# One pool of eight PSUM banks for the whole program, its banks handed out in turn, and the last gated rows split two at a time

## The chip, the cores and the metric

The kernel runs on one core of one Trainium2 chip. The metric is the device time of one execution in microseconds (us). A core has five engines with queues of their own: TensorE (PE; its weight loads are listed as PEld), VectorE (DVE), ScalarE (ACT), GpSimd (POOL) and SyncE (SP, which here only issues transfers). Matmuls write to PSUM, an accumulator memory of eight banks of 128 x 512 fp32 words; ACT and DVE read the results from there.

## The reference

Two layers over two batches of frames: a prompt of 512 frames of one new stream, and 16 new frames of each of 8 running streams (128 rows), together 640 rows of width 2048 in fp32. Layer 0 is stick-breaking attention with 16 heads of 128 (the running streams also see 512 cached frames); layer 1 is gated linear attention (GLA) with 4 heads, keys of 256 and values of 512, whose recurrent state is updated. Cut to what matters:

```
for layer i in (0, 1):
    shift, scale, gate = split(c @ w_ada[i] + b_ada[i], 3)
    h = rmsnorm(x, norm_g[i]) * (1 + scale) + shift
    i = 0:  q, k, v, z = split(h @ w_in0, 4);  o = stick_breaking(q, k, v)
            y = (o * silu(z)) @ w_out0
    i = 1:  q, k, v, r, a = split(h @ w_in1);  g = log_sigmoid(a @ w_a2 + b_a) / 16
            per chunk:  b = cumsum(g);  q_in = q * exp(b)
                        o = tril(q_in @ (k * exp(-b)).T) @ v + q_in @ S
                        S = exp(b_last) * S + (k * exp(b_last - b)).T @ v
            o = o * rsqrt(mean(o * o) + EPS) * g_out
            y = (o * silu(r)) @ w_out1
    x = x + gate * y
y = rmsnorm(x, final_norm_g)
```

The new keys and values of layer 0 and the final states of layer 1 are outputs too.

## The kernel before, in words

All large products are made with operands split in a high and a low half (fp32r): `halves` casts the high half on ACT (line 134) and subtracts it on DVE (line 135); each product is then three matmuls, high by high, high by low and low by high.

TensorE runs in the order in which the program is written (`manual_schedule(engines={PE})`); the other engines' orders come from the Tile scheduler, which plays the program in a timeline model, except in two stretches where they too are as written. What is written in which order on TensorE is decided by a small planner in the program: `Side` holds lanes (generators), and `drive` runs one piece of the main matmuls, then lets the lanes whose waiting time is over put their own matmuls between. A lane says with `step(wait, tp=, z=)` how long it waits and how many banks it takes; `pe["now"]` counts modelled time. Neither knows about real banks.

The stages, with the names that share the eight banks in each (`share_banks`):

1. adaLN and the input projection of layer 0 (`six`, `by_sevens`, matmuls on line 591; evacuations on line 597): mm=5, z=1, tp=2.
2. Attention of layer 0 (`prompt_lane`, `sample_lane`) between the matmuls of the gate projection (`plain`, line 650) and of the output projection (`share`, line 696; evacuations on lines 701 and 704): mm=2, z=2, tp=4.
3. The rest of layer 0's output projection and the input projection of layer 1: mm=5, z=1, tp=2.
4. GLA attention, again between `plain` (line 650) and `share` (line 696): mm=2, z=1, tp=5.
5. The last columns of layer 1's output projection (`hs_gemm512`, line 365, then line 2088) and the final norm: mm=8.

`bank(tag)` gives a tile of one bank. `share_banks` closes the PSUM pool of the old stage and opens another; within a pool each name is one tag with as many buffers as the stage gives it, and the scheduler chooses a free buffer for each tile.

In stage 4 three lanes run: `decays` (line 1669 matmuls), `prompt_lane` (4 heads x 4 chunks of 128 frames) and `sample_lane`. For each chunk the prompt lane takes a tp tile o and accumulates in it over several pieces (`mm3`, line 1579): attention weights by values, then two groups of query by state. Between them it takes other tp tiles: `update` (line 1579; scaled on ACT, line 1792) and `leave`, which transposes the previous chunk's output (line 1628). When o is complete, `normed` squares it on ACT (line 1604), `rstd_of` computes the root on DVE (line 232) and POOL (line 234), and `scaled_by` scales o on ACT (line 1608), which is the last read of o's bank. The sample lane accumulates in the z bank and takes a tp tile for each of 16 state updates of a head (line 1928, read on DVE, line 1930).

At the start of stage 5, six of the gated rows (kt 10 to 15) are loaded from DRAM and split; rows 8 and 9 were split in stage 4. The block of 8 rows is used in four pairs, each with a pair of weight rows, ten groups of three matmuls for each pair.

Of the kernel before, what the change touches and what calls it, by code (L numbers as in the profile page):

```python
# [8 lines left out]
F32 = mybir.dt.float32  # L9
# [6 lines left out]
P = 128  # L16
# [25 lines left out]
def hybrid_step_kernel(ctx: ExitStack, tc: tile.TileContext, A: dict, O: list):  # L42
    nc = tc.nc
    PS = bass.MemoryType.PSUM
# [9 lines left out]
    def by(l, r):  # L54

        n = r.free_size()
        if l.dtype == F32R:
            pe["now"] += n / 2400 + 0.0133
        elif l.free_size() <= 32:
            pe["now"] += n / pe["quad"] + 0.01  # L60
        else:
            pe["now"] += n / 600 + 0.005
        return r
# [6 lines left out]
    def load(out, in_):  # L70
        nc.sync.dma_start(out=out, in_=in_)

    def store(out, in_):
        nc.sync.dma_start(out=out, in_=in_)
# [10 lines left out]
    banks = ctx.enter_context(ExitStack())  # L85
# [2 lines left out]
    l0 = ExitStack()  # L88
    ad = l0.enter_context(tc.tile_pool(name="ad", bufs=1, reuse_waits="tile"))

    psum = {}

    def share_banks(**bufs):

        banks.close()
        psum["pool"] = banks.enter_context(tc.tile_pool(name="ps", bufs=1, space=PS))
        psum["bufs"] = bufs

    def bank(tag):
        return psum["pool"].tile([P, 512], F32, tag=tag, name=f"ps_{tag}", bufs=psum["bufs"][tag])  # L100

    share_banks(mm=5, z=1, tp=2)


# [28 lines left out]
    def halves(hi, lo, x, e=None):  # L133
        nc.scalar.copy(hi, x)  # L134
        (e or dve).tensor_tensor(lo, x, hi.bitcast(F32), op=ALU.subtract)  # L135
# [13 lines left out]
    def wraw(src, a, n):  # L149
        r = wp.tile([P, 1024], F32, tag="wr", name="wr", bufs=WR)[:, :a * n]  # L150
        load(r.rearrange("p (a n) -> p a n", a=a), src)
        return r
# [4 lines left out]
    def wpiece(src, a, n):  # L157

        return wsplit(wraw(src, a, n), a)
# [68 lines left out]
    def rstd_of(pool, ss, n, name):  # L228

        w = ss.shape[1]  # L230
        ms = pool.tile([P, w], F32, tag=name + "_ms", name=name + "_ms")
        dve.tensor_scalar(ms, ss, 1.0 / n, EPS, op0=ALU.mult, op1=ALU.add)
        r = pool.tile([P, w], F32, tag=name + "_r", name=name + "_r")
        nc.gpsimd.tensor_tensor(r, ms, mhalf[:, :w], op=ALU.pow)
        return r
# [26 lines left out]
    def slot(n, shape=(P, T), dt=F32R, name="h"):  # L262
        return hp.tile(list(shape), dt, tag=f"t{n}", name=name)
# [9 lines left out]
    class Side:  # L273
# [19 lines left out]
        def add(self, gen):  # L293
            self.lanes.append([gen, None])
            self.next(self.lanes[-1])
# [46 lines left out]
    side = Side()  # L342

    def drive(*gens):
        for g in gens:
            for _ in g:
                side.tick()

    def hs_gemm512(hT, w, n0, evac, mid=None, toks=range(TOK), piece=wpiece, k0=0, nk=KT):

        acc = {a: bank("mm") for a in toks}
        src = w.rearrange("(kt p) n -> p kt n", p=P)
        for pc in range(nk // 2):
            if pc == min(2, nk // 2 - 1) and mid is not None:
                mid()
            for k2 in range(2):
                hT[k0 + 2 * pc + k2]
            wh, wl = piece(src[:, k0 + 2 * pc:k0 + 2 * pc + 2, n0:n0 + 512], 2, 512)
            for a in toks:
                c = slice(P * a, P * a + P)  # L360
                for k2 in range(2):
                    kt = k0 + 2 * pc + k2
                    h, lo = hT[kt]
                    for l, r, first, last in ((h, wh, True, False), (h, wl, False, False), (lo, wh, False, True)):
                        mm(acc[a], l[:, c], by(l[:, c], r[:, k2, :]), start=kt == k0 and first,  # L365
                           stop=kt == k0 + nk - 1 and last)
                    if k2 == 0:
                        yield
                if pc == nk // 2 - 1:
                    evac(a, acc[a])  # L370
                yield

    def gate_bc(pool, i, c, bufs=2):

        g = pool.tile([P, 2, 512], F32, tag="gate_bc", name="gate_bc", bufs=bufs)
        cs = slice(512 * c, 512 * c + 512)
        load(g[:, 0, :], gate_d[i][0, cs].partition_broadcast(P))
        for b in range(NB):
            load(g[NT * b:NT * b + NT, 1, :], gate_d[i][1 + b, cs].partition_broadcast(NT))
        return g  # L380
# [542 lines left out]
    with tc.tile_pool(name="kp", bufs=2, reuse_waits="tile") as kp, \  # L923
# [12 lines left out]
        later = at.tile([P, 2], F32, name="later", bufs=1)  # L936
# [313 lines left out]
    with tc.tile_pool(name="o0", bufs=1, reuse_waits="tile") as po, ExitStack() as only_d:  # L1250
# [161 lines left out]
        r = wp.tile([P, 1024], F32, tag="wr", name="wr", bufs=WR)[:, :256].rearrange("p (k n) -> p k n", k=KT)  # L1412
# [77 lines left out]
        n = 0  # L1490
# [13 lines left out]
        r, wa2 = (rows_in.tile([P, GH * 256], t, tag=n, name=n)[:96] for n, t in (("wa2r", F32), ("wa2", F32R)))  # L1504
# [15 lines left out]
    w_out1 = A["gla_w_out"][0]  # L1520
    og1 = {}
# [499 lines left out]
    with tc.tile_pool(name="o1", bufs=1, reuse_waits="tile") as po:  # L2021
        ss4 = po.tile([P, TOK, 4], F32, name="ss4f")
        gf = po.tile([P, D], F32, name="gf")
        ring3["pool"] = po
        for kt in range(10, 16):
            r = po.tile([P, T], F32, tag="rows", name="og_in", bufs=6)
            load(r, og_d[kt // 4][:, kt % 4, :])
            n = 20 + 2 * kt % 12
            og1[kt] = [slot(n + e) if kt < 14 else po.tile([P, T], F32R, name=f"og{e}{kt}") for e in range(2)]
            halves(*og1[kt], r)  # L2030
        got = {}

        def fetch_x1(c):
            if c == 0:
                load(gf, A["final_norm_g"].partition_broadcast(P))
            xs = []
            for a in range(TOK):
                xs.append(po.tile([P, 512], F32, tag="xc", name="x1", bufs=8))
                load(xs[a], x1_d[a][:, 512 * c:512 * c + 512])
            got[c] = xs, gate_bc(po, 1, c)  # L2040

        def add(a, c, pt):
            cs = slice(512 * c, 512 * c + 512)
            xs, g = got[c]
            y = y_t[a, c]
            dve.tensor_tensor(y, pt, y, op=ALU.add)
            dve.tensor_tensor(y, y, g[:, a // 4, :], op=ALU.mult)
            dve.tensor_tensor(y, y, xs[a], op=ALU.add)
            junk = po.tile([P, 512], BF16, tag="junk", name="junk", bufs=1)
            act(junk, y, AF.Square, accum_out=ss4[:, a, c:c + 1])  # L2050
            if c < 3:
                dve.tensor_tensor(y, y, gf[:, cs], op=ALU.mult)
                return
            ss = po.tile([P, 1], F32, tag="ssf", name="ssf", bufs=2)
            dve.tensor_reduce(out=ss, in_=ss4[:, a, :], axis=mybir.AxisListType.X, op=ALU.add)
            r = rstd_of(po, ss, D, "fin")
            dst = y_p[0, P * a:P * a + P, :] if a < 4 else y_s.rearrange("b t d -> (b t) d")
            dve.scalar_tensor_tensor(y, y, r, gf[:, cs], op0=ALU.mult, op1=ALU.mult)
            store(dst[:, cs], y)
            for n in range(3):  # L2060
                x = y_t[a, n]
                if n < 2:
                    act(x, x, AF.Copy, scale=r)
                else:
                    dve.tensor_scalar(x, x, r, None, op0=ALU.mult)
                store(dst[:, 512 * n:512 * n + 512], x)

        def piece(src, a, n):
            t = parts.pop(0) if parts else split(first.pop(0)) if first else None
            return [x.rearrange("p (a n) -> p a n", a=2) for x in t] if t else wpiece(src, a, n)  # L2070

        kept = []
        for c in range(3):
            drive(hs_gemm512(og1, w_out1, 512 * c, lambda a, pt: add(a, c, pt), lambda: fetch_x1(c), piece=piece,
                             k0=8, nk=8))
        for i in range(4):
            r = wraw(w_of(2 + i // 2, 3, i % 2), 2, 512)
            h, lo = (po.tile([P, 1024], F32R, name=f"{n}{i}") for n in ("kh", "kl"))
            halves(h, lo, r)
            kept.append([t.rearrange("p (a n) -> p a n", a=2) for t in (h, lo)])  # L2080
        fetch_x1(3)
        for a in range(TOK):
            acc = bank("mm")
            for n in range(8):
                wh, wl = kept[n // 2]
                h, lo = (x[:, P * a:P * a + P] for x in og1[8 + n])
                for l, r, start, stop in ((h, wh, True, False), (h, wl, False, False), (lo, wh, False, True)):
                    mm(acc, l, by(l, r[:, n % 2, :]), start=n == 0 and start, stop=n == 7 and stop)  # L2088
            add(a, 3, acc)
# [27 lines left out]
```

## Time and profile before

| what | value |
|---|---|
| time, median of 3 runs | 2473.24 us (2471.8 to 2477.05) |
| time of the profiled execution | 2472.03 us |
| its span, first to last instruction | 2470.1 us |
| granted TensorE clock | 0.995 of full speed |
| busy: PE, PEld | 2408.5 us (98%), 2141.9 us (87%) |
| busy: DVE, ACT, POOL | 1581.7 us (64%), 993.3 us (40%), 156.6 us (6%) |
| HBM read, written | 410.05 MB, 89.13 MB |

The stages in the profiled execution run from 0 to about 919, to 1386, to 1945, to 2348 and to 2470 us. Columns of rows of the timeline: start in us, duration in us, engine, source line, operation, tiles as out<-in, shapes and count; in brackets the engine's idle time before the row and what ended it. Rows of the view of stretches give the length, the busy time and instruction count of PE, PEld, DVE, ACT and POOL, then the granted clock, the share of time of the transfer engines, and GB/s. Buffer numbers are left out of names: all tiles of one name look alike.

### The profile page before, as it was taken

What the parts mean: (1) busy time and instruction counts of PE and PEld (TensorE: products, weight loads), DVE (VectorE), ACT (ScalarE), POOL (GpSimd) and SP (SyncE); (2) the same over time, 40 slices, a digit from 0 to 9 for tenths busy, and PEclk for the clock granted to TensorE, in tenths of its full rate; (3) what the DMA queues carried; (4) which work ended last, traced back from release to release, by engine and by line L of the source; (5) the groups of instructions that cost most, each with busy time, mean ns of one, the idle gap of its engine ahead of it and who ended that gap; (6) DMA issues with size and microseconds to landing.
All of it is one profiled execution on the core that took longest, in us unless ns stands there. A gap on an engine that the chain in (4) does not pass through costs nothing.

```text
span 2470.1 us, 44598 instructions
## 1 busy us (share of the span) xinstructions
PE 2408.5 (98%) x17817; PEld 2141.9 (87%) x17817; DVE 1581.7 (64%) x2580; ACT 993.3 (40%) x1711; POOL 156.6 (6%) x405
## 2 busy tenths in 40 slices
PE   7999999999999999999999999999999999999998
PEld 4689999999999999888887767999999989977776
DVE  5765655555556656766776578766676566676556
ACT  4432222222223335555544245433333555565223
POOL 0010000000000000000000010000000132332000
PEclk8999999999999999999999999999999999999999
DMA  9966666766664348777774564444434678976634
GB/s 344 370 218 213 210 216 199 239 210 225 210 197 128 109 145 274 259 241 235 254 235 147 187 234 129 136 123 125 134 111 114 175 247 264 303 261 224 220 115 149
DMA packets 477841, 502.12 MB, mean 203 GB/s; under 512 B 26618, under 2 KB 386434, under 8 KB 477506
## 3 DMA queue, kind: packets, MB, share of 16 engines
q1 hardware_dynamic: 449042, 440.80, 56.2%
q0 software_dynamic: 14432, 46.67, 5.5%
q10 hardware_dynamic: 14160, 11.80, 1.4%
q8 instruction: 140, 2.29, 0.4%
q14 instruction: 67, 0.55, 0.1%
HBM read 410.05 MB, written 89.13 MB: 202 GB/s over the span
## 4 chain that ended last, share of the span: by engine, by line
PE 85%; DVE 4%; ACT 3%; DMA 2%; issue 1%; POOL 0%; SPq 0%; ACTq 0%; POOLq 0%; DVEq 0%
PE ps_mm L591 43%; PE ps_mm L696 11%; PE ps_mm L650 10%; PE ps_mm L365 3%; PE ps_tp L1100 2%; PE ps_tp L1579 2%; PE ps_tp L1152 1%; PE ps_tp L1056 1%; PE ps_z L1032 1%; PE ps_z L180 1%; PE ps_mm L2088 1%; PE ps_z L1114 1%; PE ps_z L222 1%; PE ps_tp L677 1%; PE ps_mm L515 1%
## 5 line engine op out<-in xcount | busy, mean ns | idle before, releaser
L591 PE MATMUL ps_mm<-sums,wh 128*128 128x320 f32 x2752 | 613.6, 311 | 1.5 <-ACT wh L134 1.5
L591 PEld LDWEIGHTS ps_mm<-sums,wh 128*128 128x128 f32 x2752 | 458.0, 188 | 10.4 <-issue 7.4
L591 PE MATMUL ps_mm<-h,wh 128*128 128x320 f32 x2064 | 461.4, 311 | 0.8 <-DVE u L597 0.8
L591 PE MATMUL ps_mm<-sums,wl 128*128 128x320 f32 x1376 | 425.2, 309 | 0.7 <-DVE wl L135 0.7
L135 DVE TENSOR_TENSOR wl<-wr,wh 128x1024 fp32r<-128x1024 f32 x193 | 236.2, 1225 | 211.1 <-ACT wh L134 208.1
L591 PEld LDWEIGHTS ps_mm<-h,wh 128*128 128x128 f32 x2064 | 343.2, 188 | 15.7 <-issue 11.0
L134 ACT CAST wh<-wb 128x1024 fp32r<-128x1024 f32 x170 | 178.4, 1049 | 431.8 <-PE ps_mm L591 368.2
L134 ACT CAST wh<-wr 128x1024 fp32r<-128x1024 f32 x193 | 202.5, 1050 | 324.8 <-PE ps_mm L591 186.8
L591 PE MATMUL ps_mm<-h,wl 128*128 128x320 f32 x1032 | 318.9, 309 | 0.0
L650 PE MATMUL ps_mm<-h,wh 128*128 128x320 f32 x1152 | 263.5, 316 | 3.5 <-DVE out L597 2.4
L591 PEld LDWEIGHTS ps_mm<-sums,wl 128*128 128x128 f32 x1376 | 258.3, 188 | 1.0 <-DVE wl L135 1.0
L135 DVE TENSOR_TENSOR wl<-wb,wh 128x1024 fp32r<-128x1024 f32 x170 | 207.8, 1222 | 51.0 <-ACT wh L134 50.6
L650 PEld LDWEIGHTS ps_mm<-h,wh 128*128 128x128 f32 x1152 | 192.0, 188 | 17.9 <-issue 8.9
L696 PE MATMUL ps_mm<-wh,ogh 128*128 128x512 f32 x450 | 196.8, 437 | 6.2 <-ACT y L704 3.0
L591 PEld LDWEIGHTS ps_mm<-h,wl 128*128 128x128 f32 x1032 | 193.8, 188 | 0.0
L650 PE MATMUL ps_mm<-h,wl 128*128 128x320 f32 x576 | 177.9, 309 | 0.0
L696 PE MATMUL ps_mm<-wh,ogl 128*128 128x512 f32 x450 | 177.0, 393 | 0.3 <-DVE ogl L135 0.3
L696 PE MATMUL ps_mm<-wl,ogh 128*128 128x512 f32 x450 | 177.0, 393 | 0.2 <-DVE wl L135 0.2
L696 PEld LDWEIGHTS ps_mm<-wh,ogh 128*128 128x128 f32 x450 | 84.9, 189 | 34.4 <-issue 15.1
L650 PEld LDWEIGHTS ps_mm<-h,wl 128*128 128x128 f32 x576 | 108.2, 188 | 0.0
L696 PEld LDWEIGHTS ps_mm<-wh,ogl 128*128 128x128 f32 x450 | 84.5, 188 | 20.2 <-DVE ogl L135 0.7
L515 PE MATMUL ps_mm<-wh,h 128*128 128x512 f32 x252 | 90.7, 415 | 5.6 <-ACT h L134 4.0
(370 smaller groups left out, 3719.6 us busy)
## 6 DMA issues: line engine op xcount, KB each, us to landing
ar<-in_w_ada_dram SPq DMA_DIRECT2D x128, 512.0 KB
wb<-in_sb_w_in_dram SPq DMA_DIRECT2D x82, 512.0 KB
ar<-in_w_ada_dram SPq DMA_DIRECT2D x128, 256.0 KB
kc<-in_cache_sb_k_dram SPq DMA_DIRECT2D x64, 512.0 KB
vc<-in_cache_sb_v_dram SPq DMA_DIRECT2D x64, 512.0 KB
wr<-in_gla_w_in_dram SPq DMA_DIRECT2D x51, 512.0 KB
wb<-in_gla_w_in_dram SPq DMA_DIRECT2D x45, 512.0 KB
wr<-in_sb_w_in_dram SPq DMA_DIRECT2D x44, 512.0 KB
```

What stands on the lines that cost most here:

```text
L134: nc.scalar.copy(hi, x)
L135: (e or dve).tensor_tensor(lo, x, hi.bitcast(F32), op=ALU.subtract)
L180: mm(acc[32 * q:32 * q + 32, :w], cT[:, kt + m, :], by(cT[:, kt + m, :], rs[m // each][:, m % each, q, :]), start=kt + m == 0, stop=kt + m ...
L222: mm(acc[32 * j:32 * j + 32, :256], cT[:, kt + m, :], by(cT[:, kt + m, :], r[:, 256 * j:256 * j + 256]), start=kt + m == 0, stop=kt + m == ...
L365: mm(acc[a], l[:, c], by(l[:, c], r[:, k2, :]), start=kt == k0 and first, stop=kt == k0 + nk - 1 and last)
L515: mm(acc[a], l, by(l, r[:, e, :]), start=j == 0 and e == 0 and begun, stop=j == 7 and e == 1 and last)
L591: mm(acc, l[:, k, :], by(l[:, k, :], r), start=start and k == 0 and first, stop=k == 7 and last, skip_group_check=True)
L650: mm(acc[nt], l[:, k, :], by(l[:, k, :], r), start=k0 == 8 and k == 0 and first, stop=k0 == 0 and k == 7 and last)
L677: turn_block(tp[:, c:c + P], block(out[hh][:, t0:t0 + P]), ident)
L696: mm(acc, l, by(l, r[:, e, :]), start=i == 0 and e == 0 and first, stop=i == 1 and e == 1 and last)
L1100: turn_block(tp[:, P * c:P * c + P], block(kc[:, c, P * hh:P * hh + P]), ident)
L1579: mm(out, l[a], by(l[a], r[b]), start=start and n == 0, stop=stop and n == 2, skip_group_check=True)
```

## The change

The PSUM pool is opened once, before the first stage, and never closed. It has eight tags, b0 to b7, of one buffer each. `psum["last"]` holds the banks in the order of their last use, the one used longest ago first. `share_banks` only gives each name so many banks, from the front of that list, and `bank(tag)` takes the name's banks in turn. In stage 5 the loads of the six rows stay where they are; two rows are split there, and two more after the fifth and after the fifteenth group of three matmuls of the first block. The other steps of the loop are as in `drive`.

```diff
-    psum = {}
+    psum = {"pool": banks.enter_context(tc.tile_pool(name="ps", bufs=1, space=PS)), "last": list(range(8)), "of": {}}
 
     def share_banks(**bufs):
 
-        banks.close()
-        psum["pool"] = banks.enter_context(tc.tile_pool(name="ps", bufs=1, space=PS))
-        psum["bufs"] = bufs
+        free = list(psum["last"])
+        psum["of"] = {tag: [free.pop(0) for _ in range(n)] for tag, n in bufs.items()}
 
     def bank(tag):
-        return psum["pool"].tile([P, 512], F32, tag=tag, name=f"ps_{tag}", bufs=psum["bufs"][tag])
+        own = psum["of"][tag]
+        own.append(own.pop(0))
+        psum["last"].remove(own[-1])
+        psum["last"].append(own[-1])
+        return psum["pool"].tile([P, 512], F32, tag=f"b{own[-1]}", name=f"ps_{tag}")
...
         ring3["pool"] = po
+        later = []
         for kt in range(10, 16):
             r = po.tile([P, T], F32, tag="rows", name="og_in", bufs=6)
             load(r, og_d[kt // 4][:, kt % 4, :])
             n = 20 + 2 * kt % 12
             og1[kt] = [slot(n + e) if kt < 14 else po.tile([P, T], F32R, name=f"og{e}{kt}") for e in range(2)]
-            halves(*og1[kt], r)
+            later.append((og1[kt], r))
+
+        def next_rows():
+            for _ in range(2):
+                if later:
+                    two, r = later.pop(0)
+                    halves(*two, r)
+
+        next_rows()
...
         for c in range(3):
-            drive(hs_gemm512(og1, w_out1, 512 * c, lambda a, pt: add(a, c, pt), lambda: fetch_x1(c), piece=piece,
-                             k0=8, nk=8))
+            for n, _ in enumerate(hs_gemm512(og1, w_out1, 512 * c, lambda a, pt: add(a, c, pt), lambda: fetch_x1(c),
+                                             piece=piece, k0=8, nk=8)):
+                if n % 10 == 4:
+                    next_rows()
+                side.tick()
```

## The prediction

> **What bounds the kernel now.** I read the page first (shares, then the chain that ended last), then the busy time by stage, then the timeline of TensorE around each change of stage and around the accumulators of the last-but-one stage.
>
> ```profile
> span 2470.1 us, 44598 instructions
> PE 2408.5 (98%) x17817; PEld 2141.9 (87%) x17817; DVE 1581.7 (64%) x2580; ACT 993.3 (40%) x1711; POOL 156.6 (6%) x405
> PE 85%; DVE 4%; ACT 3%; DMA 2%; issue 1%; POOL 0%; SPq 0%; ACTq 0%; POOLq 0%; DVEq 0%
> ...
> 1945.20:2347.70 402.50, 396.39 (x2292) 341.19 (x2292) 244.93 (x420) 210.96 (x389) 99.57 (x181) 1.00 0.77 250
> ```
>
> TensorE is the bound: it is busy 2408.5 of 2470.1 us. It runs in the order in which the program is written, so a wait at its head stops everything behind it, and a microsecond of waiting is a microsecond of time unless a later wait shrinks by as much. The last row is the GLA attention stage (time, then busy time of PE, PEld, DVE, ACT, POOL): PE stands for 402.50 - 396.39 = 6.1 us there. The change adds and removes no matmul, no transfer and no vector work. It can only move waits, and those are of two kinds: the waits at the four changes of stage, and the waits for a bank inside a stage.
>
> **The change, part 1: the pool is not closed at a change of stage.**
>
> ```profile
> 921.04 0.53 PE L650 MATMUL ps_mm<-h,wh 128*128 128x320 f32 x2 [1.75 <-DVE out L597]
> ...
> 1387.04 0.47 PE L696 MATMUL ps_mm<-wh,ogh 128*128 128x512 f32 x1 [0.88 <-DVE y L701]
> ...
> 1945.86 0.53 PE L650 MATMUL ps_mm<-h,wh 128*128 128x320 f32 x2 [0.68 <-DVE out L597]
> ...
> 2349.36 0.47 PE L365 MATMUL ps_mm<-wh,ogh 128*128 128x512 f32 x1 [1.47 <-DVE y L701]
> ...
> 1386.81 1.22 DVE L135 TENSOR_TENSOR s<-wr,s 128x1024 fp32r<-128x1024 f32 x1
> ...
> 1388.49 0.62 PE L696 MATMUL ps_mm<-s,ogh 128*128 128x512 f32 x2
> ```
>
> Columns of these rows: start, us, engine, line, tiles; in brackets the idle time before it and what ended it. Each is the first matmul of a new stage, and each waits for the last read of the old stage's last bank. With one pool, share_banks hands the names the banks used longest ago first, so the first matmul finds a bank that was read long before. I remove all four waits, 1.75 + 0.88 + 0.68 + 1.47 = 4.8 us, and ask what is late next. At the second change it is a weight: the low half "s" is ready at 1386.81 + 1.22 = 1388.03, and its matmul is the eighth of the stage, at about 1388.7 now (the row at 1388.49 holds the seventh and another). So about 0.6 us of the 0.88 remain. At the other three I know of no late operand: the first weights are split several microseconds before. I take 4.5 us; ends 0 (another operand is late at each) and 4.8.
>
> **Part 2: which bank a tile gets inside a stage.** Before, a name such as tp had five buffers of one tag, and a new tile could have whichever was free. After, bank() takes the names' banks strictly in turn, each a tag with one buffer. For tiles that are used for the same short time nothing changes. In the GLA attention stage one tile is not short: the prompt lane's output accumulator "o" (name tp, L1579), which lives over three later groups of matmuls, the square, the power on POOL and the scaling on ACT (L1608), and only then is free. With tp=5 taken in turn, the fifth tp tile after o gets o's bank, whatever else is free. How that falls for one o:
>
> ```profile
> 2176.96 0.62 PE L1579 MATMUL ps_tp<-v,aTh 128*128 128x512 f32 x2
> ...
> 2178.35 0.39 PE L1928 MATMUL ps_tp<-vst,kst 128*128 128x512 f32 x1
> ...
> 2179.45 0.62 PE L1579 MATMUL ps_tp<-v,krh 128*128 128x512 f32 x2
> ...
> 2180.14 0.40 PE L1928 MATMUL ps_tp<-vst,kst 128*128 128x512 f32 x1
> ...
> 2183.78 0.39 PE L1579 MATMUL ps_tp<-S1h,qcl 128*128 128x512 f32 x1
> 2184.01 0.39 PE L1928 MATMUL ps_tp<-vst,kst 128*128 128x512 f32 x1
> ...
> 2185.13 0.49 PE L1628 MATMUL ps_tp<-ident,on 128*128 128x128 f32 x3
> ...
> 2188.10 0.57 POOL L234 TENSOR_TENSOR on_r<-on_ms,mhalf 128x1 f32<-128x1 f32 x1
> ...
> 2190.46 0.69 ACT L1608 ACTIVATE on<-ps_tp,on_r 128x512 f32<-128x512 f32 x1
> ```
>
> o opens at 2176.96 and gets its last matmul at 2183.78. The next tp tiles open at 2178.35, 2179.45, 2180.14, 2184.01 and 2185.13: the fifth is the transpose of L1628. It starts now without a wait, although o is read until 2190.46 + 0.69 = 2191.15, so it has another bank now. In turn it would stand 2191.15 - 2185.13 = 6.0 us, and on TensorE all of L1628, the sample lane's L1928 and the filler matmuls of L650 or L696 stand behind it; ACT, DVE and POOL wait for their outputs.
>
> I went through the 16 o's of the prompt lane so, counting five tp tiles on from each. Eight of the 16 (heads x chunks) meet their own release. The first and the last of the eight:
>
> ```profile
> 2008.27 0.39 PE L1579 MATMUL ps_tp<-S1h,qcl 128*128 128x512 f32 x1
> ...
> 2011.15 0.62 PE L1579 MATMUL ps_tp<-v,krh 128*128 128x512 f32 x2
> ...
> 2011.67 0.69 ACT L1608 ACTIVATE on<-ps_tp,on_r 128x512 f32<-128x512 f32 x1
> ...
> 2265.44 0.39 PE L1579 MATMUL ps_tp<-S1h,qcl 128*128 128x512 f32 x1
> ...
> 2266.95 0.48 PE L1928 MATMUL ps_tp<-vst,kst 128*128 128x512 f32 x1
> ...
> 2269.00 0.69 ACT L1608 ACTIVATE on<-ps_tp,on_r 128x512 f32<-128x512 f32 x1
> ```
>
> With today's releases the eight waits would be 1.2, 5.1, 1.8, 1.0, 3.7, 4.5, 6.0 and 2.7 us, in sum 26.0, at 2011, 2023, 2038, 2084, 2097, 2109, 2185 and 2267 us. That is the upper end. The release can come earlier than today, because a standing TensorE sends ACT, DVE and POOL no new work, and their queues are filled in another order when the wait is known. The hold, from the end of o's last matmul to the end of L1608, is 3.7 us in the first of the rows, 3.9 in the last, 7.0 in the long one. The shortest in the stage:
>
> ```profile
> 1993.87 0.39 PE L1579 MATMUL ps_tp<-v,aTl 128*128 128x512 f32 x1
> ...
> 1995.85 0.69 ACT L1608 ACTIVATE on<-ps_tp,on_r 128x512 f32<-128x512 f32 x1 [0.87 <-POOL on_r L234]
> ```
>
> There it is 1996.54 - 1994.26 = 2.3 us. From o's last matmul to the fifth tile are 2.5, -0.2, 3.5, 2.5, 0.9, 0.7, 0.9 and 1.1 us in the eight, so a hold of 2.3 us everywhere would leave waits of 0, 2.5, 0, 0, 1.4, 1.6, 1.4 and 1.2, in sum 8: the lower end. I take a hold of 3.8 us, that of the first and last rows, in which little but the chain itself stands: 1.3 + 4.0 + 0.3 + 1.3 + 2.9 + 3.1 + 2.9 + 2.7 = 18.5 us. The z accumulator of the sample lane has its own bank as before; the mm banks were taken in turn of release before and stay near that. In the other stages I find no tile that would come before its bank is read, so nothing is charged there.
>
> What might shrink by as much: after a stall ACT and DVE have caught up, so later waits of PE in this stage can be shorter. They are small:
>
> ```profile
> PE ps_mm L696 <- ACT y L704: 3.0, 3, 1.9
> ...
> PE ps_mm L650 <- ACT pl L1539: 1.0, 1, 1.0
> ```
>
> (Us in total, times, longest.) I give back 1 us of these 4; ends 0 and 4.
>
> **The clock after a stall.** One long stall is in the trace:
>
> ```profile
> 1466.81 0.50 PE L515 MATMUL ps_mm<-wh,h 128*128 128x512 f32 x1 [3.03 <-ACT h L134]
> ...
> 1468.00:1471.40 3.40, 3.40 (x8) 2.68 (x9) 2.64 (x9) 0.90 (x3) 0.55 (x1) 0.51 0.09 34
> 1471.40:1475.40 4.00, 4.00 (x21) 3.06 (x20) 3.39 (x8) 3.54 (x10) 0.00 (x0) 1.00 0.13 45
> ```
>
> After 3.03 us of idle the granted clock is 0.51 for 3.4 us, in which 8 matmuls start, against 21 in the 4.0 us behind: the slow 3.4 us cost about 1.6 us (at 0.5 of the clock half of the time is lost, at most 1.7). The 1.75 us of idle at 921 caused no such row. Of my eight stalls, five are 2.7 to 4.0 us; I charge two such drops, 3.2 us; ends 0 and 8 (five). The Trainium skill, TensorE: Matmul & The Clock Gate, Part 1, states a free-running activity window of about 3.4 us, after an idle one of which the clock halves. The drop's length in the trace agrees, though its idle time was a little shorter than that; by the page's rule read strictly only my one stall of 4.0 us would drop the clock, and the sum would be 1.6 us lower.
>
> **Part 3: the last gated rows two at a time.** Rows 10 and 11 are split (one ACT cast and one DVE subtraction for each row) where all six were; rows 12 to 15 are written into the first column block, after groups 5 and 15. No instruction is added. They are needed at the third and fourth weight pair. In the block, matmuls of the second pair begin at 2356.28, those of the third about 6.8 us later, and DVE idles between:
>
> ```profile
> 2356.28 0.39 PE L365 MATMUL ps_mm<-wh,h 128*128 128x512 f32 x1
> ...
> 2357.57 1.23 DVE L135 TENSOR_TENSOR wl<-wr,wh 128x1024 fp32r<-128x1024 f32 x1 [6.49 <-ACT wh L134]
> ```
>
> A pair of rows costs under 2 us on each engine, inside 6.49 us of DVE's idle time, so I charge 0; without that cover it would be at most 2 us. No queue is moved past a transfer: the six loads stay where they are.
>
> **The sum**, against the profiled execution's own 2472.03 us (span 2470.1; the median of the three runs is 2473.24, 1.2 above): -4.5 + 18.5 + 3.2 - 1 = +16.2, so 2488.2 profiled and about 2489 us in the median, slower by 0.65%.
>
> **Rivals.**
> - *Only the first part shows: the waits inside the stage do not come.* For it: the change keeps every count of banks, and the removed waits are plain in four rows. It decides if o's release can come 3 us sooner than in the rows, at less than a 1 us hold, or if the bank in turn is not o's. Against it: a hold of 2.3 us is the shortest seen. Time: 2473.2 - 4.5 = 2468.7, less 0.18%; up to 2467 if caught-up engines shorten further waits. This is faster or, by the bound of 0.2% (4.9 us, about what a measurement of this kernel can tell from no change), the same. 0.14.
> - *Short holds:* the eight waits come at the lower end, without a drop of the clock: -4.5 + 8 - 1 = +2.5, 2476 us, the same within 0.2%. It decides if the holds fall below 2.6 us. For it: only the chain square, DVE, POOL, ACT is then queued. Against it: POOL's queue holds transfers for the state in front of the power, which wait for landings, not for TensorE. 0.10.
> - *Full holds and the clock:* today's releases and five drops: -4.5 + 26 + 8 = +29.5, 2503 us. The queues of ACT and POOL keep today's order. 0.13.
> - *The change of stage gains nothing* since another operand is late at each: +20.7, 2494 us. 0.05.
>
> **How the numbers follow.** The forecast as summed has the remaining 0.58. Predicted: 2489. The range reaches from the short holds with a margin to most of the full ones, 2473 to 2501, and leaves out the first rival and the far end of the third, about 0.2; the forecast's own range, from the choices of hold between 3 and 4.6 us, is 2481 to 2496. Slower by over 0.2%: forecast 0.58, third 0.13, fourth 0.05, together 0.76. Within 0.2%: short holds 0.10 and half of the first rival, 0.17 in all. Faster: 0.07.
>
> **What would show it.** Right: in the timeline the first matmuls of L650 (twice), L696 and L365 start with no idle time behind L597 and L701; in the waits of PE in the GLA attention stage new rows ps_tp (L1628, L1928, L1579) waiting for ACT on L1608, eight or so, 1 to 6 us each; the stage takes some 16 to 20 us longer; granted clock below 1.00 in slices behind the longest. Wrong: no row of PE waiting for L1608, or the stage's PE idle time still near 6 us; or a new wait in the last stage on the split rows (L365 behind ACT og or h), which would make part 3 cost.

## The result, and the profile after

The changed kernel is slower: 2504.34 us in the median (2500.42 to 2505.31) against 2474.55 us for the kernel before beside it (2471.80 to 2477.05), a ratio of 1.0119 with an interval of [1.0104, 1.0133]. The forecast was 2489 us with a range to 2501: the sign and the eight waits came as said, the size did not. The profiled execution of the changed kernel took 2503.78 us, its span is 2501.7 us (31.6 more than before), its granted clock 0.988 (0.995 before). TensorE's order is the same in both, matmul for matmul, so the delay can be read at each of the 17817 matmuls. At the end of the GLA attention stage it is already over 30 us. Line numbers of the changed kernel are three higher here: L1608 of before is L1611, L1628 is L1631.

The GLA attention stage, from its first matmul (L650, then L653) to the first of the last stage (L365, then L368), in the view of stretches, before and after:

```profile
1945.86:2349.36 403.50, 396.58 (x2293) 341.20 (x2293) 245.87 (x422) 212.51 (x391) 99.57 (x181) 1.00 0.77 249
```
```profile
1945.49:2381.09 435.60, 405.60 (x2295) 347.45 (x2293) 245.74 (x421) 212.08 (x391) 101.16 (x181) 0.98 0.73 231
```

The stage is 435.60 - 403.50 = 32.1 us longer, and the row splits that in two. TensorE is idle for 30.00 us where it was idle for 6.92 (23.1 more), and the same matmuls keep it busy 9.0 us longer, at a granted clock of 0.98. What it waited for (us in total, times, longest):

```profile
PE ps_tp L1631 <- ACT on L1611: 10.4, 3, 5.2
PE ps_tp L1931 <- ACT on L1611: 7.3, 2, 4.7
PE ps_tp L1900 <- DVE kc L1895: 3.9, 1, 3.9
PE ps_tp L1582 <- ACT on L1611: 3.6, 3, 1.7
PE ps_mm L699 <- DVE y L704: 1.5, 4, 0.7
PE ps_mm L699 <- ACT y L707: 1.5, 2, 1.1
...
PE ps_tp L1594 <- DVE k L1698: 0.8, 1, 0.8
```

The three rows that end on L1611, the scaling of o, are new: eight waits, 21.3 us. In the timeline they stand at the eight matmuls that the forecast named, and at no other:

```profile
2011.99 0.50 PE L1582 MATMUL ps_tp<-v,krh 128*128 128x512 f32 x1 [1.10 <-ACT on L1611]
...
2028.71 0.80 PE L1931 MATMUL ps_tp<-vst,kst 128*128 128x512 f32 x1 [4.70 <-ACT on L1611]
...
2047.28 0.50 PE L1582 MATMUL ps_tp<-v,krh 128*128 128x512 f32 x1 [1.66 <-ACT on L1611]
...
2095.76 0.50 PE L1582 MATMUL ps_tp<-v,krh 128*128 128x512 f32 x1 [0.87 <-ACT on L1611]
...
2112.59 0.69 PE L1631 MATMUL ps_tp<-ident,on 128*128 128x128 f32 x2 [3.68 <-ACT on L1611]
...
2129.38 0.44 PE L1631 MATMUL ps_tp<-ident,on 128*128 128x128 f32 x2 [1.53 <-ACT on L1611]
...
2210.71 0.69 PE L1631 MATMUL ps_tp<-ident,on 128*128 128x128 f32 x2 [5.19 <-ACT on L1611]
...
2300.61 0.50 PE L1931 MATMUL ps_tp<-vst,kst 128*128 128x512 f32 x1 [2.58 <-ACT on L1611]
```

Four stretches run at half of the clock, three behind the long ones of these waits and the last behind the wait for kc:

```profile
2026.20:2033.00 6.80, 4.29 (x16) 4.15 (x17) 1.44 (x3) 0.69 (x1) 2.74 (x5) 0.50 0.91 302
2111.50:2118.30 6.80, 5.71 (x22) 3.71 (x22) 1.90 (x3) 1.35 (x2) 1.92 (x4) 0.50 0.92 278
2210.50:2213.90 3.40, 3.19 (x12) 3.10 (x13) 2.18 (x3) 0.15 (x1) 0.86 (x2) 0.50 0.51 173
2227.60:2231.00 3.40, 3.40 (x10) 2.62 (x9) 2.94 (x6) 2.17 (x4) 1.32 (x2) 0.50 1.01 358
```

TensorE is busy 4.29 + 5.71 + 3.19 + 3.40 = 16.6 us in them; half of that, 8.3 us, is lost, and makes up nearly all of the 9.0 us of longer busy time.

The changes of stage came right too: the first matmuls of the four later stages carry no bracket now, and one new wait follows the first of them:

```profile
920.82 0.46 PE L653 MATMUL ps_mm<-h,wh 128*128 128x320 f32 x2
...
930.37 0.42 PE L653 MATMUL ps_mm<-h,wl 128*128 128x320 f32 x1 [1.18 <-DVE wl L138]
...
1387.01 0.39 PE L699 MATMUL ps_mm<-wh,ogh 128*128 128x512 f32 x1
...
1945.49 0.46 PE L653 MATMUL ps_mm<-h,wh 128*128 128x320 f32 x2
...
2381.09 0.39 PE L368 MATMUL ps_mm<-wh,ogh 128*128 128x512 f32 x1
```

So far this is a coincidence of places and of times. That the turn causes the loss, and what makes a wait long, took experiments.

### The profile page after: what moved, and what is told of

The parts are those of the page before. It is cut to its first block, busy times and chain, and to the rows that moved or that the text cites. A ratio compares the mean times of both kernels' runs of the same rounds, so it can differ in the third digit from the quotient of the medians.

```text
span 2501.7 us, 44596 instructions
## 1 busy us (share of the span) xinstructions
PE 2419.7 (97%) x17817; PEld 2151.4 (86%) x17817; DVE 1582.8 (63%) x2580; ACT 994.4 (40%) x1711; POOL 157.9 (6%) x405
## 4 chain that ended last, share of the span: by engine, by line
PE 81%; DMA 4%; DVE 4%; ACT 3%; issue 2%; POOL 0%; SPq 0%; ACTq 0%; POOLq 0%; DVEq 0%
PE ps_mm L594 42%; PE ps_mm L699 10%; PE ps_mm L653 8%; PE ps_mm L368 3%; PE ps_tp L1103 2%; PE ps_tp L1582 2%; PE ps_tp L1155 1%; PE ps_tp L1059 1%; PE ps_z L1035 1%; PE ps_z L183 1%; PE ps_mm L518 1%; PE ps_mm L2103 1%; PE ps_z L1117 1%; PE ps_z L225 1%; PE ps_tp L680 1%
## 5 line engine op out<-in xcount | busy, mean ns | idle before, releaser
L594 PEld LDWEIGHTS ps_mm<-sums,wh 128*128 128x128 f32 x2752 | 458.2, 188 | 10.4 <-issue 7.4
L653 PE MATMUL ps_mm<-h,wh 128*128 128x320 f32 x1152 | 265.7, 318 | 1.0 <-ACT pl L1542 1.0
L653 PEld LDWEIGHTS ps_mm<-h,wh 128*128 128x128 f32 x1152 | 194.3, 190 | 15.7 <-issue 8.7
L699 PE MATMUL ps_mm<-wh,ogh 128*128 128x512 f32 x450 | 197.2, 438 | 4.1 <-DVE y L704 2.2
L653 PE MATMUL ps_mm<-h,wl 128*128 128x320 f32 x576 | 179.1, 311 | 1.2 <-DVE wl L138 1.2
L699 PE MATMUL ps_mm<-wh,ogl 128*128 128x512 f32 x450 | 177.5, 394 | 0.3 <-DVE ogl L138 0.3
L699 PE MATMUL ps_mm<-wl,ogh 128*128 128x512 f32 x450 | 177.4, 394 | 0.0
L699 PEld LDWEIGHTS ps_mm<-wh,ogh 128*128 128x128 f32 x450 | 85.3, 190 | 31.2 <-issue 13.3
L653 PEld LDWEIGHTS ps_mm<-h,wl 128*128 128x128 f32 x576 | 109.3, 190 | 1.4 <-DVE wl L138 1.4
L699 PEld LDWEIGHTS ps_mm<-wh,ogl 128*128 128x128 f32 x450 | 84.8, 188 | 20.4 <-DVE ogl L138 0.7
```

The source lines that it names most:

```text
L594: mm(acc, l[:, k, :], by(l[:, k, :], r), start=start and k == 0 and first, stop=k == 7 and last, skip_group_check=True)
L653: mm(acc[nt], l[:, k, :], by(l[:, k, :], r), start=k0 == 8 and k == 0 and first, stop=k0 == 0 and k == 7 and last)
L699: mm(acc, l, by(l, r[:, e, :]), start=i == 0 and e == 0 and first, stop=i == 1 and e == 1 and last)
```

## The experiments

The theory: the loss comes from banks handed out in turn, which meet the bank that o holds. Rival 1: the pool that lives for the whole program, or the moved splits, cost. Rival 2: the other order that the scheduler gave to ScalarE, VectorE and GpSimd costs, and the bank waits are only its sign. All ratios are against the kernel before, run beside on the same chip. "Stage" is the length of the GLA attention stage between the same two matmuls as above, "idle" TensorE's idle time in it, "scaling" its waits for the scaling of o, and for the copy where there is one.

| kernel | median, us | before beside it, us | ratio, interval | stage, us | idle, us | scaling, us |
|---|---|---|---|---|---|---|
| before | | | | 403.5 | 6.9 | 0 |
| changed | 2504.34 | 2474.55 | 1.0119 [1.0104, 1.0133] | 435.6 | 30.0 | 21.3 |
| rows only | 2476.74 | 2476.52 | 1.0002 [0.9993, 1.0012] | 405.6 | 7.2 | 0 |
| turn, pool reopened | 2505.55 | 2476.52 | 1.0123 [1.0108, 1.0139] | 435.3 | 32.0 | 24.3 |
| o out of the turn | 2474.90 | 2476.52 | 0.9998 [0.9988, 1.0007] | 404.7 | 6.2 | 0 |
| o copied out | 2475.10 | 2476.52 | 0.9993 [0.9982, 1.0004] | 408.8 | 9.8 | 3.1 |
| four long holds out | 2478.69 | 2476.23 | 1.0010 [0.9999, 1.0022] | 411.6 | 11.5 | 6.7 |
| four short holds out | 2495.86 | 2476.23 | 1.0080 [1.0058, 1.0101] | 426.0 | 21.4 | 14.3 |
| turn, no state stores | 2489.79 | 2475.25 | 1.0057 [1.0040, 1.0074] | 422.5 | 20.3 | 15.2 |
| o out of the turn, no state stores | 2472.56 | 2475.25 | 0.9985 [0.9975, 0.9995] | 404.9 | 6.9 | 0 |

**The rows alone.** The kernel before, with the new loop that splits the rows:

```diff
-            halves(*og1[kt], r)
+            later.append((og1[kt], r))
...
+                if n % 10 == 4:
+                    next_rows()
```

> The kernel before with only the last gated rows split two at a time; its banks are shared as before. Theory (the loss comes from banks handed out in turn, which meet the bank that the tile o holds): nothing of the loss is here, 2474 us, within 0.2% of the kernel before. Rival (the moved splits cost): part of the 29.8 us shows here, which would be over 2480 us.

Measured: 1.0002 [0.9993, 1.0012]. The moved splits neither cost nor bring anything that can be measured; the half of rival 1 that names them falls.

**The turn, with the pool closed and opened again.** Banks in turn as in the changed kernel, rows as before, and

```diff
     def share_banks(**bufs):
+        banks.close()
+        psum["pool"] = banks.enter_context(tc.tile_pool(name="ps", bufs=1, space=PS))
         free = list(psum["last"])
```

> The banks are handed out in turn as in the changed kernel, but the pool is closed and opened again at each change of stage, and the rows are split as before. Theory: the eight waits on o's bank stay, the 4 to 5 us that the changes of stage gave go: 2508 us, and matrix work waits for the scaling of o in the stage of gated attention about 22 us as in the changed kernel. Rival 1 (a pool that lives for the whole program, or the rows, is what costs): 2474 us.

Measured: 1.0123, 29 us slower than before, with neither the long-lived pool nor the moved rows in it. Rival 1 falls. Against the changed kernel I expected 4 us more and got 1.2, within the intervals of both. Its waits in the GLA attention stage:

```profile
PE ps_tp L1633 <- ACT on L1613: 13.8, 3, 8.6
PE ps_tp L1933 <- ACT on L1613: 6.9, 2, 4.8
PE ps_tp L1584 <- ACT on L1613: 3.6, 3, 1.7
PE ps_tp L1902 <- DVE kc L1897: 1.4, 1, 1.4
```

The same eight, with one of 8.6 us where the changed kernel has 5.2 and then 3.9 for kc: the two sums, 10.0 and 9.1 us, differ less than their parts. That looks like one disturbance paid at two places, but no run shows it.

**o out of the turn.** The changed kernel, where o's bank is not handed on before its last read is written:

```diff
+    def bank_kept(tag):
+        n = psum["of"][tag].pop(0)
+        return take(tag, n), lambda: psum["of"][tag].append(n)
...
-                o = bank("tp")
+                o, give_back = bank_kept("tp")
...
                 left = u, scaled_by(*on)
+                give_back()
```

> The changed kernel, but a tile o takes its bank out of the turn until its last read, the scaling, is written: the turn goes over the other banks. Theory: the eight waits on o's bank go, with them the halved clock after them and most of the new waits on other engines; the gains at the changes of stage stay: 2469 to 2471 us, faster than both kernels. Rival 1 (the pool for the whole program or the rows cost): about 2500 us. Rival 2 (the order that other engines' work got is what costs, with the bank waits as its sign): the waits on the scaling go, waits on other work take their place, over 2485 us.

Its row of the stage, and TensorE's waits in it:

```profile
1948.36:2353.01 404.65, 398.46 (x2294) 342.47 (x2293) 245.13 (x421) 211.32 (x391) 99.51 (x181) 1.00 0.77 249
```
```profile
PE ps_mm L707 <- ACT y L715: 2.4, 2, 1.9
PE ps_mm L707 <- DVE y L712: 1.4, 4, 0.6
```

All eight waits are gone, so are the wait for kc and 29.4 us of the time; the stage is 31 us shorter. Rival 2 fares ill: where the bank is not waited for, the other engines' work does not cost either. It is not excluded by this alone, since the scheduler plans the other engines anew in each variant, and no run keeps the changed kernel's order without its waits. But the 4 to 5 us of the changes of stage that I expected on top do not show: 0.9998 [0.9988, 1.0007] allows a gain of 3.0 us at most. This version does not beat the kernel before.

**o copied out of its bank.** ScalarE copies o as soon as it is complete; the square and the scaling read the copy:

```diff
-            act(on, o, AF.Square, accum_out=s1)
-            return on, rstd_of(gl, s1, 512, "on"), o
+            act(on, o, AF.Copy)
+            junk = gl.tile([P, 512], mybir.dt.bfloat16, tag="junk", name="junk", bufs=1)
+            act(junk, on, AF.Square, accum_out=s1)
+            return on, rstd_of(gl, s1, 512, "on"), on
```

> The changed kernel, but ScalarE copies o out of its bank as soon as it is complete, and the square and the scaling read the copy: the bank is held for one copy instead of until the scaling, at the price of one more ScalarE instruction of about 0.6 us for each o. Theory (the hold's length is what is paid): about 3 us come off each of the eight waits, which leaves some 5 of 22.7 us and one drop of the clock at most: 2474 to 2482 us. Rival 2 (the order of work on ScalarE and VectorE costs): no better than 2495 us, since ScalarE has more work than before. Rival 1: about 2504 us.

TensorE's waits in the stage (L1607 is the copy, L1613 the scaling):

```profile
PE ps_tp L1633 <- ACT on L1613: 2.3, 1, 2.3
...
PE ps_tp L1933 <- ACT on L1607: 0.8, 1, 0.8
```

Banks are still taken in turn, and 0.8 us of waiting for a bank is left (the 2.3 us on L1613 come at the transposes that read its result). ScalarE works 10.4 us more in the stage (222.45 against 212.08) and the kernel is 29 us faster than the changed one, which speaks against rival 2: more work on ScalarE costs nothing like the order of the banks. It is the length of the hold that is paid.

**Four of the eight at a time.** Of the sixteen o's only four take their bank out of the turn: first the four whose next user waits longest by the tiles of the kernel before (third, seventh, eighth and eleventh; in the changed kernel 4.70, 3.68, 1.53 and 5.19 us), then the other four of the eight (second, fourth, sixth and fifteenth; 1.10, 1.66, 0.87 and 2.58 us).

```diff
-                o, give_back = bank_kept("tp")
+                out_of_turn["n"] += 1
+                o, give_back = bank_kept("tp") if out_of_turn["n"] in (3, 7, 8, 11) else (bank("tp"), lambda: None)
```

> As the run in which every o takes its bank out of the turn, but only four of the sixteen do: those whose next user waited 4.86, 3.84, 1.69 and 5.35 us. Going through the tiles of the kernel before, the four short waits stay at their places (0.98, 1.22, 1.76 and 2.75 us, 6.7 in all) and no new one comes. Theory with a cost behind long waits (the halved clock and the disordered queues follow waits of some 4 us and more): no halved clock in the stage, no 3.9 us wait of the transposes of kc, 2475 + 6.7 less what is absorbed: 2479 to 2482 us. Rival (every wait on a held bank has its share of what follows): 13 us of follow-ups by share of the waits, 4 of them here: 2484 to 2487 us.

> The other four of the eight take their bank out of the turn, those whose next user waited 1.27, 1.81, 1.03 and 2.83 us; the four long waits stay at their places, 19.3 us by the tiles of the kernel before, 15.7 as they came in the changed kernel. Theory with a cost behind long waits: the halved clock and the wait for kc stay with them, 2504 - 6.9 = 2497 us, granted clock 0.98 in the stage. Rival (every wait has its share of what follows): 2504 - 6.9 - 4 = 2493 us. If this and the run with the four long ones out lose together what the changed kernel loses (about 30 us), the waits add up.

With the long ones out, the row of the stage and, behind it, of a stretch inside it:

```profile
1942.12:2353.73 411.61, 400.10 (x2294) 343.60 (x2293) 245.13 (x421) 211.37 (x391) 100.57 (x181) 0.99 0.75 245
...
2272.40:2275.80 3.40, 3.40 (x10) 2.65 (x9) 1.35 (x2) 1.25 (x2) 1.09 (x2) 0.50 0.80 223
```

With the short ones out, the stage:

```profile
1943.85:2369.84 425.99, 404.57 (x2295) 347.85 (x2293) 245.72 (x421) 211.27 (x391) 99.85 (x181) 0.98 0.74 237
```

Against the run with every o out (404.65 us), the four short waits and a new one of 0.4 us, together 6.7 us, make the stage 7.0 us longer, and the four long ones of 14.3 us make it 21.3 us longer. Together that is 28.3 of the changed kernel's 31.0 us: in the traces the waits nearly add up (in the medians 2.5 and 19.6 against 29.8, of which two or three us may be the spread of the runs). The price differs: about 1.05 us for each us of short waits, 1.5 for long ones. The first median, 2478.69 us, is just under the 2479 to 2482 us of the theory of a cost behind long waits. The second, 2495.86, lies between the theory's 2497 and the rival's 2493, and kc waits 1.6 us there, not the 3.9 that were to stay: the two runs favour the theory and do not settle it. Its line between long and short is wrong, too. No halved stretch was expected among the short waits, and there are two: the row at 2272.40, behind a wait of 2.58 us, and one at 2231.46, where runs without any wait for a bank have one as well. What draws the line instead is in the last section.

**GpSimd's queue.** What makes a hold long? In the changed kernel's timeline, VectorE's, GpSimd's and ScalarE's rows between o's last matmul and its scaling, at the wait of 4.70 us:

```profile
2024.91 0.15 DVE L235 TENSOR_SCALAR on_ms<-oss 128x1 f32<-128x1 f32 x1
...
2025.03 0.54 POOL L78 DMA_DIRECT2D out_dram<-s  x1 [1.71 <-DVE qcl L138]
2026.82 0.54 POOL L78 DMA_DIRECT2D s<-in_state_gla_dram  x1 [1.25 <-DMA out_dram<-s]
2027.37 0.57 POOL L237 TENSOR_TENSOR on_r<-on_ms,mhalf 128x1 f32<-128x1 f32 x1
...
2027.97 0.69 ACT L1611 ACTIVATE on<-ps_tp,on_r 128x512 f32<-128x512 f32 x1 [2.55 <-POOL on_r L237]
```

The operand of the power is there at 2025.06. The power starts at 2027.37, since two transfers stand ahead of it in GpSimd's queue, and the second waits 1.25 us for the landing of an earlier store, whose buffer it reuses. To test it, the stores of the running streams' final states are left out, in the changed kernel and, as a control, in the one with o out of the turn:

```diff
         def leaves(x):
             h, e, dt, m = x
-            move(ss_o[0, 2 * m + e, h, P * dt:P * dt + P, :], states.pop(x)[0])
+            states.pop(x)
```

> The changed kernel without the 64 transfers that store the running streams' final states from GpSimd's queue (these outputs are left out): the state loads in that queue then wait for no landing of a store, and the power for a chunk's root does not stand behind them. Theory (GpSimd's queue is what makes a hold of o longer than its chain): in the changed kernel the power starts 2.3 us after its operand at 2024.91 + 0.15, 0.9 us after that at 2109.07, 3.4 us after that at 2205.68 and 0.9 us after that at 2297.93; these go, except where ScalarE stands for a weight's transfer (the cast before the scaling at 2209.97), so the waits on the scaling fall from 21.3 to between 12 and 15 us, and with less of the halved clock the time falls by 8 to 13 us, to 2491 to 2496 us. Rival (the holds are set by ScalarE's order, or by TensorE's standing): the waits stay at 19 to 22 us and the time at 2501 to 2505 us.

> The control for the run before: the kernel in which every o takes its bank out of the turn, also without the 64 stores of the running streams' final states. No hold is waited for there, so both theories expect what that kernel had with the stores, 2473 to 2476 us; what it differs by is what the left-out transfers are worth by themselves, and is to be taken off the other run.

With banks in turn and no such stores, TensorE's waits on the scaling, and the power at the place of the 4.70 us:

```profile
PE ps_tp L1631 <- ACT on L1611: 6.1, 3, 2.3
PE ps_tp L1931 <- ACT on L1611: 5.5, 2, 3.4
PE ps_tp L1582 <- ACT on L1611: 3.6, 3, 1.6
```
```profile
2022.18 1.03 POOL L237 TENSOR_TENSOR on_r<-on_ms,mhalf 128x1 f32<-128x1 f32 x1
```

The waits on the scaling fall to 15.2 us, just above what I expected and well below the rival's 19; the time, 2489.79 us, is just below what I expected. Which ones fall says more: 4.70 becomes 3.4 and the 5.19 is now at most 2.3, while the group of three short ones (L1582) keeps its 3.6. The kernel's loss is 0.57% where it was 1.19%. The left-out stores by themselves are worth 0.15% [0.05, 0.25] in the control, so about 12 us, give or take some 6 by the three intervals, come from the holds and from what follows them, and the wait for kc is gone too. The stores made the long holds longer. How much of that is the place of the power in GpSimd's queue, these two runs do not tell. At the 5.19 us ScalarE stood as well, ahead of the scaling, for a weight's transfer:

```profile
2209.02 1.04 ACT L137 CAST wh<-wr 128x1024 fp32r<-128x1024 f32 x1 [3.21 <-DMA wr<-in_gla_w_out_dram]
```

ScalarE was through with that cast at about 2210.0, GpSimd with the power already at 2209.80. Without the stores that cast comes behind the scaling and waits 0.15 us for its transfer. And at the 4.70 us 3.4 remain although the power starts 0.5 us after its operand: that part is the chain itself.

## Why the prediction was wrong in size and right in kind

Step by step, against the profiled executions (span +31.6 us, forecast +16.2). Of the 15.4 us between the two, the clock has 5.8, new waits that were put at nothing 4.7, the eight waits 2.8 and the changes of stage 1.2; 0.2 came off with what was given back, and 1.1 belong to no term:

- **Changes of stage, forecast -4.5:** all four waits went. The low weight at the second change was late as said, but by 0.3 us, not 0.6. At the first change I named no late operand, and there was one: nine microseconds in, TensorE stands 1.18 us for VectorE's wl (row at 930.37), and so it does, for 0.9 to 1.2 us, in every variant with one pool. Net -3.3. In the time it cannot be seen: with the eight waits taken away, the ratio is 0.9998.
- **Eight waits on o's bank, forecast +18.5:** all eight came at the named matmuls, 21.3 us. The sum was 2.8 us short. The single hold of 3.8 us that I took for all misjudged them one by one: it gave 4.0, 2.9 and 2.9 us to the three long ones, which took 4.70, 3.68 and 5.19, 0.3 to the one at 2038, which took 1.66, and 3.1 to the one at 2109, which took 1.53. Today's releases, the upper end, were nearer one by one: seven of the eight within 0.9 us. Their sum of 26.0 is further off, for the sake of one: the sixth was to wait 4.5 us and waited 1.53, since there the power now starts 0.37 us after its operand, and no transfer ahead of it holds it up. So the nearness of 18.5 to 21.3 is in part luck. The transfers in GpSimd's queue I had named, but as an argument against short holds only. (The low end of the forecast's own range is off as well: by the same sum holds of 3 us give some 2483 us, not 2481.)
- **The clock, forecast +3.2 with ends 0 and 8:** this is the step that failed most, 9.0 us of longer busy time. I charged two drops of 3.4 us, by the length of the stalls; the trace has four halved stretches of together 20.4 us, two of them 6.8 us long and one behind the wait for kc, which was no stall of mine. What counts is how much of a wait falls into one window of 3.41 us of a fixed grid (last section): the waits of 4.70 and 3.68 us, 2.19 + 2.51 and 2.62 + 1.06 us by windows, halved two windows each, and the one of 5.19 a single one. Not all of it is the banks': the runs with the rows alone and with o out of the turn each have a stretch of 3.4 us at half clock near 2231 us, and are busy about 1.8 us longer than the profiled execution of before, which has none in the stage. So about 7 us belong to the change. The reading of the Trainium skill (TensorE: Matmul & The Clock Gate, Part 1) by which only an idle time of a whole window counts was weighed as making my sum smaller; the traces do not agree with it: a stretch of half clock stands behind an idle time of 2.58 us (the row at 2272.40), and the window in the Trainium skill is about 3.4.
- **New waits behind the stalls, forecast none:** 3.9 us for kc and 0.8 for k. The chain of the first, in the changed kernel's rows:

```profile
2217.61 8.22 SPq L71 DMA_DIRECT2D og_in<-og  x2
...
2223.91 0.72 ACT L137 CAST ogh<-og_in 128x640 fp32r<-128x640 f32 x1 [4.89 <-DMA og_in<-og]
...
2225.12 0.29 ACT L1894 CAST kc<-kd 128x128 fp32r<-128x128 f32 x1
...
2226.41 0.44 PE L1900 MATMUL ps_tp<-ident,kc 128*128 128x128 f32 x2 [3.90 <-DVE kc L1895]
```

  In the kernel before the first load of that stretch was issued at 2188.32 and ScalarE's cast of it stood behind the cast of kc:

```profile
2193.34 0.29 ACT L1891 CAST kc<-kd 128x128 fp32r<-128x128 f32 x1
2195.59 0.73 ACT L134 CAST ogh<-og_in 128x640 fp32r<-128x640 f32 x1 [1.97 <-DMA og_in<-og]
```

  Now it stands ahead, waits 4.89 us for its transfer, and kc with it. "In another order when the wait is known" was in the forecast as a reason for shorter holds; here it made a second wait.
- **Given back, forecast -1:** the waits of L699 fell from 4.2 to 3.0 us, -1.2.
- **The rows, forecast 0:** 1.0002 [0.9993, 1.0012].

In sum -3.3 + 21.3 + 9.0 + 4.7 - 1.2 = +30.5 of 31.6; the other microsecond was there at the end of the first stage (the delay is 1.7 us at its last matmul), where the two programs are alike. The time is that of the third rival, full holds and the clock (2503 us, 0.13), with a smaller part for the holds than it had and the kc wait for the rest, so that the agreement is in part luck. Its condition, that the queues of ACT and POOL keep today's order, did not hold for ACT, as the rows for kc show.

What stays open: how much of the kc wait is the late transfer and how much the place of the cast in ScalarE's order, since no run changed one without the other; and how much of the long holds is GpSimd's queue alone.

## What to carry to other kernels

A bank handed out in turn is only as good as its slowest user: the planner here counts free banks, the turn gives a particular one, and a tile that lives over several later tiles of its name has to be taken out of the turn (here 29.4 us) or emptied early. Price a stall of TensorE above its length once it passes some 1.9 us: four waits of together 14.3 us cost 21.3. Up to some 3.8 us it depends on where the windows fall; a longer stall always puts 1.9 us into one window, and half of TensorE's work in the next is lost (an estimate from the borders below). And ask of each link of a hold what stands ahead of it in its queue: a 0.57 us power waited 2.3 us behind transfers that had nothing to do with it.

## What the hardware showed beyond expectation

The granted clock goes by a fixed grid of windows of 3.41 us. In the changed kernel's trace the four halved stretches start at 2026.20, 2111.53, 2210.52 and 2227.59 us, which is 25, 29 and 5 times 3.413 us from one to the next, and each is one or two windows long. What counts is how long TensorE stands inside one window, not how long a wait is. The GLA attention stages of the ten profiled executions, cut along this grid, have 1191 windows at full clock. Behind each of the 20 with 1.89 us or more of idle time the next window ran at half; behind none of the 1171 with 1.73 us or less did it. A halved window with 1.06 us or more of idle time was followed by another (6 times), one with 0.61 us or less was not (20 times). Elsewhere in the program the border is less sharp: windows with 1.4 to 1.8 us of idle time went either way.

So the same wait can cost a halved window or not. L696 waits 1.92 us for ScalarE in the kernel before, with a border of the grid inside the wait:

```profile
2229.77 0.50 PE L696 MATMUL ps_mm<-wh,ogh 128*128 128x512 f32 x1 [1.92 <-ACT y L704]
```
```profile
2225.69:2229.10 3.41, 2.14 (x9) 1.09 (x7) 1.59 (x4) 2.82 (x7) 1.63 (x3) 1.00 1.06 225
2229.10:2232.51 3.41, 2.74 (x12) 2.28 (x13) 2.49 (x6) 2.48 (x5) 1.08 (x2) 1.00 1.04 363
```

The run with the rows alone has the same wait of 1.92 us inside one window:

```profile
2227.51:2230.92 3.41, 1.53 (x7) 1.26 (x8) 2.10 (x5) 2.30 (x5) 1.08 (x2) 1.00 1.02 295
2230.92:2234.33 3.41, 3.41 (x10) 2.63 (x9) 2.20 (x4) 1.63 (x2) 0.54 (x1) 0.50 1.06 403
```

The wait of 2.58 us likewise: in the changed kernel it falls into two windows (1.24 and 1.34 us) and the clock stays, in the run with the four long holds out it lies in one, and the next is halved.
